# Bonus sums of the RWKV recurrence: both heads and two chunks in one matrix product, in a two-layer trunk on one core

## The chip, the core and the metric

The kernel runs on one core of a Trainium2 chip. A core has a matrix engine (TensorE, PE in the profile; its weight loads are listed apart as PEld), a vector engine (DVE), a scalar engine (ACT), GpSimd (POOL), and DMA queues, here issued by SyncE (SP). The engines run their own instruction lists and wait for each other by semaphores. The metric is the device time of one execution in microseconds (us); lower is better.

## The reference, cut to what matters

A trunk of two layers over 1024 tokens of 1024 features, all in 32-bit floats. Layer 1 is RWKV-7 time mixing, layer 2 a diagonal state-space mixer (S5) with a gated output; each is followed by a dense MLP with 4096 hidden features and a squared ReLU, and each of the four sub-layers ends in a layer norm over `sqrt(2) * h + f(h)`. The change touches one term of the first, the bonus:

```
r, k, v = xr @ wr, xk @ wk, xv @ wv          # xr, xk, ...: x mixed with the token before
kk = heads(k * k_k); kk = kk / max(norm(kk), 1e-12)
k  = k * (1.0 + (a - 1.0) * k_a)             # a: sigmoid of a low-rank product
...
state = state * w_t + (state @ a_t) b_t' + v_t k_t'      # one 64 x 64 state per head, token by token
o_t   = state @ r_t
...
o = group_norm(o) * lnx_g + lnx_b
bonus = sum(rh * kh * r_k, axis=-1, keepdims=True) * vh  # one number per token and head, times v
o = o + bonus
return (o * g) @ wo
```

There are 16 heads of 64 features. The bonus needs, for each of 1024 tokens and 16 heads, one sum over 64 features.

## The kernel before, in words

Activations lie with the features on the 128 partitions (eight tiles of 128) and 512 tokens along the free dimension. The tokens are worked in two halves H = 0 and 1. Every large product is made of three (`mm3`, L204): the high parts of weight and operand, high by low and low by high; `split` makes the high part on ACT (L155) and the low part on DVE (L156). This is the bulk of PE's work: first the projections of both halves (`rwkv_proj`), whose results go to DRAM as `scr["r"]`, `scr["k"]`, `scr["sg"]`, `scr["a"]`, `scr["g"]` and `scr["v"]`, then for H = 0 the output projection `wo(0)`, the first layer norm, and the MLP; then `wo(1)` and so on for H = 1, and the layers behind.

Beside the bulk runs the recurrence, in eight units m = 0 to 7. A unit holds 256 tokens (four chunks of 64) and eight heads (512 features, half q = m % 2), as two pairs of feature tiles, j = 0 and 1. For each unit:

- `elem(m)` loads k, sg, a and r of its tokens (tiles `ldk`, `ldsg`, `lda`, `ldr`), 128 features by 2 x 256 tokens for each j. It squares `kk` on ACT (L549, L550), sums over each head on PE (`pss`, L553), turns the inverse norms back with four transposes (`pn`, L561), runs the scan of the log decays on DVE (L564), two exponentials on ACT, and forms `kf`, `AR` and `KB` (L573 to L584). Then POOL multiplies `kf` by r, and PE makes the **bonus sums** `pb` (L590) with `rksel`, a table that holds r_k of the first head of a tile in its first column, zero on the other head's partitions, and that of the second head in its second column. One DVE copy (L592) takes them to `bo`.
- `amat` makes the products of a chunk's vectors among each other (`pA`, L614), `kbtrans` transposes `KB` (`pT`), `invert` solves the 64 x 64 triangles, and `chain` passes the state from chunk to chunk (`pR`, `pX`, `pU`, `pO`, L718 to L745).
- `gnorm` normalises the result and adds the bonus: POOL multiplies v by `bo` into `vt` (L781) and adds. The sums are thus read one unit later than they are made.

In `bo` the four chunks of the unit lie along the free dimension, beside the four feature tiles; the 64 tokens of a chunk lie on 64 partitions, the upper 64 for the first head of a tile and the lower 64 for the second.

Two PSUM banks (pool `pa`) serve `pss`, `pn`, `pb` and `pA` in turn; three (`pd`) serve the bulk products, two (`pc`) the chain, one (`pl`) the layer norms and `invert`.

**What sets the order.** The engines' lists are fixed when the program is built. Each part gets a base rank (`with rank(...)`): the units m * 10000 with offsets of `RK`, the bulk of half 0 and 1 100000, `wo(0)` 99000, the first layer norm -1. A scheduler goes through all of them with an estimate of each instruction's time and takes at every step what is ready with the lowest rank. So an edit in `elem` can shift every instruction behind it on every engine.

**Other places that the text speaks of.** The first layer norm (`layer_norm` with `by_pe`, half 0): DVE subtracts the mean `pm` from eight tiles `hA` (L927), ACT squares them (L874), PE sums the squares (`pq`), POOL and ACT make the scale `rb` (L896), PE turns it (`pr`, L899), DVE scales (L881) and the parts `oAh` and `oAl` go to the MLP. Behind the first MLP's blocks, `yload(1)` splits the recurrence's result `yl` into `oBh` and `oBl` (L156) for `wo(1)`, the second output projection, whose sums are added to `hB` (L1018); DVE also makes the tables of layer 2 (`s5_tables`, `turns`, L1170 to L1271) there, and adds the MLP's output sums to `hA` (L1050).

Of the kernel before, what the change touches and what calls it, by code (L numbers as in the profile page):

```python
# [20 lines left out]
L = 64  # L21
# [52 lines left out]
def trunk(ctx, tc, A):  # L74
    nc = tc.nc
    V, S, G, PE, SP = nc.vector, nc.scalar, nc.gpsimd, nc.tensor, nc.sync
# [39 lines left out]
    def vec(n, k):  # L116
        i = PV.index(n)
        return pv[:, i, k : k + 1]
# [7 lines left out]
    rksel = kp.tile([128, KT, 2], F32, name="rksel")  # L126
# [393 lines left out]
    def elem(m):  # L520
        D = Unit()
        D.m, D.H, D.q, D.t0 = m, m // 4, m % 2, (m // 2) * 256
        D.KB, D.AR, D.o, D.vsa = [], [], {}, {}
        D.bo = kp.tile([128, NC, NP], F32, tag="bo", name="bo", bufs=3)
        D.PL = kp.tile([128, NC, NP], F32, tag="PL", name="PL", bufs=3)
        for j in range(2):
            n0 = 4 * D.q + 2 * j
            ld = {}
            for nm in ("k", "sg", "a", "r"):
                t = kp.tile([128, 512], F32, tag="ld" + nm, name="ld" + nm, bufs=EB[3] if nm in EB[4] else 1)  # L530
                SP.dma_start(t.rearrange("p (i t) -> p i t", i=2),
                             scr[nm][n0 * 128 : n0 * 128 + 256, D.t0 : D.t0 + 256].rearrange("(i p) t -> p i t", p=128))
                ld[nm] = t
            r, k, cs, a = ld["r"], ld["k"], ld["sg"], ld["a"]

            def v3(t):
                return t.rearrange("p (c l) -> p c l", l=L)

            def per(i):
                return slice(256 * i, 256 * i + 256)  # L540

            def ci(t):
                return t[:, :, 2 * j : 2 * j + 2].rearrange("p c i -> p i c")


            sq = kp.tile([128, HT], F32, tag="sq", name="sq", bufs=EB[0])
            kk = kp.tile([128, HT], F32, tag="kk", name="kk", bufs=EB[1])
            for i in range(2):
                S.mul(kk[:, per(i)], k[:, per(i)], vec("k_k", n0 + i))  # L549
            S.activation(sq, kk, AF.Square)  # L550
            ps = pa.tile([128, HT], F32, tag="a", name="pss")
            for tt in range(4):
                PE.matmul(ps[:, tt * 2 : tt * 2 + 2], sq[:, tt * 128 : (tt + 1) * 128], hsel, start=True, stop=True)  # L553
            rn = kp.tile([128, 8], F32, tag="rn", name="rn", bufs=2)
            V.tensor_scalar(rn, ps[:, 0:8], 1e-24, None, op0=ALU.max)
            G.tensor_tensor(rn, rn, mhalf[:, 0:8], op=ALU.pow)
            rnb = sq.rearrange("p (t h n) -> p t h n", t=4, h=2)
            S.copy(rnb, rn.rearrange("p (t h) -> p t h", h=2).unsqueeze(3).broadcast_to([128, 4, 2, 64]))
            pn = pa.tile([128, HT], F32, tag="a", name="pn")
            for tt in range(4):  # L560
                PE.transpose(pn[:, tt * 128 : (tt + 1) * 128], sq[:, tt * 128 : (tt + 1) * 128], ident)  # L561
            V.tensor_mul(kk, kk, pn)

            V.tensor_tensor_scan(cs, cmask.rearrange("p c l -> p (c l)"), cs, 0.0, op0=ALU.mult, op1=ALU.add)  # L564
            E = kp.tile([128, 8, L + 1], F32, tag="E", name="E", bufs=EB[5])
            G.memset(E[:, :, 0:1], 1.0)
            S.activation(E[:, :, 1:], v3(cs), AF.Exp, scale=-DECAY)
            V.tensor_copy(ci(D.PL), E[:, :, L].rearrange("p (i c) -> p i c", i=2))
            S.activation(cs, cs, AF.Exp, scale=DECAY)

            kf = kp.tile([128, HT], F32, tag="kf", name="kf", bufs=EB[2])
            for i in range(2):
                S.activation(kf[:, per(i)], a[:, per(i)], AF.Identity, bias=kam[:, n0 + i : n0 + i + 1],  # L573
                             scale=kah[:, n0 + i : n0 + i + 1])
            G.tensor_mul(kf, kf, k)
            ar = kp.tile([128, 8, 2, L], F32, tag="AR", name="AR", bufs=ARB)
            kb = kp.tile([128, 8, 2, L], F32, tag="KB", name="KB", bufs=KBB)
            V.tensor_mul(ar[:, :, 1], v3(r), E[:, :, 1:])
            V.scalar_tensor_tensor(ar[:, :, 0], v3(kk), -1.0, E[:, :, 0:L], op0=ALU.mult, op1=ALU.mult)
            V.scalar_tensor_tensor(a, a, 1.0, kk, op0=ALU.add, op1=ALU.mult)  # L580
            for h in range(2):
                hs = slice(64 * h, 64 * h + 64)
                V.tensor_mul(kb[hs, :, 1 - h], v3(kf)[hs], v3(cs)[hs])
                V.scalar_tensor_tensor(kb[hs, :, h], v3(a)[hs], 0.5, v3(cs)[hs], op0=ALU.mult, op1=ALU.mult)  # L584
            G.tensor_mul(kf, kf, r)
            pb = pa.tile([128, HT], F32, tag="a", name="pb")
            for c in range(8):
                for h in range(2):
                    hs, bs = slice(64 * h, 64 * h + 64), slice(64 * (1 - h), 64 * (1 - h) + 64)
                    PE.matmul(pb[bs, c : c + 1], kf[hs, c * L : (c + 1) * L], rksel[hs, n0 + c // 4, h : h + 1],  # L590
                              start=True, stop=True)
            V.tensor_copy(ci(D.bo), pb[:, 0:8].rearrange("p (i c) -> p i c", i=2))  # L592
            D.KB.append(kb)
            D.AR.append(ar)
        return D
# [213 lines left out]
    def core():  # L809
# [4 lines left out]
        with rank(3000):  # L814
            cur = elem(0)
# [6 lines left out]
        for m in range(8):  # L822
# [13 lines left out]
            if m < 7:  # L836
                with rank(base + RK[1]):
                    nxt = elem(m + 1)
# [800 lines left out]
```

## Time and profile before

| what | value |
|---|---|
| three runs | 2599.53, 2601.27, 2612.87 us; median 2601.27 |
| profiled execution, its own time | 2606.15 us |
| its span, first to last instruction | 2604.40 us |
| mean granted clock of TensorE | 0.970 |
| busy: ACT, POOL | 1206.7 us (46%), 400.0 us (15%) |
| bonus products `pb` in the program | 256, in 16 groups of 16 |

All times of single instructions come from the profiled execution. The span is cut into stretches by what the bulk does: up to about 800 us it is the projections, the first output projection and the start of the first MLP block, with the recurrence beside them; to 1030 us the first MLP with the end of the recurrence; to 1300 us the end of that MLP, the second output projection and the tables; then layer 2's half of the work. A busy share says what an engine did, not who waited; for that the chain that ended last and the idle time of a stretch are read together.

### The profile page before, as it was taken

The numbers are of one execution on the slowest core, as the hardware profiler recorded it, in microseconds if no ns is written. First come the engines' busy times: TensorE is split into PE (matmuls) and PEld (weight loads), VectorE is DVE, ScalarE is ACT, GpSimd is POOL, SyncE is SP. The second block draws the span as 40 slices with busy tenths as digits, with TensorE's granted clock in tenths as the row PEclk, the third lists the DMA queues.
The fourth block names the chain that finished last, engine by engine and source line by source line (L and its number), as shares of the span: only waits on it lengthen the run. The fifth ranks groups of instructions, "written<-read, shape, count | busy, mean of one in ns | idle before, by whom it ended". The sixth has DMA issues, their size and how long they took to land.

```text
span 2604.4 us, 43848 instructions
## 1 busy us (share of the span) xinstructions
PE 2478.2 (95%) x16684; PEld 2011.6 (77%) x16684; DVE 1809.7 (69%) x3473; ACT 1206.7 (46%) x2155; POOL 400.0 (15%) x334
## 2 busy tenths in 40 slices
PE   7989989999989999999999999999999999999997
PEld 5778767788767888777777888887777888888876
DVE  7467687578786776999886555776586555555576
ACT  7555575454454443345544333433464333433344
POOL 3110431332211102001000000100212111111011
PEclk9989989999889999999999999999999999999998
DMA  4765555565222324445565333254222111111123
GB/s 149 255 199 175 163 193 182 179 189 156 89 73 76 104 86 130 139 133 155 165 222 173 98 97 94 93 183 140 88 87 76 53 49 49 57 49 53 53 93 114
DMA packets 206290, 319.68 MB, mean 123 GB/s; under 512 B 20096, under 2 KB 80640, under 8 KB 206080
## 3 DMA queue, kind: packets, MB, share of 16 engines
q1 hardware_dynamic: 204928, 314.79, 38.5%
q8 instruction: 131, 2.15, 0.4%
q10 hardware_dynamic: 1152, 2.10, 0.2%
q14 instruction: 79, 0.65, 0.1%
HBM read 252.85 MB, written 63.96 MB: 122 GB/s over the span
## 4 chain that ended last, share of the span: by engine, by line
PE 69%; DVE 14%; DMA 8%; ACT 5%; issue 3%; POOL 1%; SPq 1%; ACTq 0%; DVEq 0%; POOLq 0%
PE d L204 51%; PE d L1087 9%; DVE wlo L156 2%; DMA wraw<-in_mw_dram 2%; PE pA L614 1%; DMA ldsg<-s_sg 1%; ACT whi L155 1%; DVE oAl L156 1%; PE pR L722 1%; PE pq L876 1%; DVE xh L660 1%; DMA s_r<-ev 0%; DMA wraw<-in_glu_dram 0%; DVE KB L584 0%; PE pu L1358 0%
## 5 line engine op out<-in xcount | busy, mean ns | idle before, releaser
L155 ACT CAST whi<-wraw 128x512 fp32r<-128x512 f32 x492 | 304.6, 620 | 646.5 <-PE d L204 426.8
L156 DVE TENSOR_TENSOR wlo<-wraw,whi 128x512 fp32r<-128x512 f32 x492 | 357.2, 727 | 250.6 <-ACT whi L155 245.6
L204 PE MATMUL d<-qbuf,whi 128*128 128x512 f32 (+1 forms) x1344 | 409.7, 387 | 11.4 <-DVE hA L1050 5.7
L204 PE MATMUL d<-oAh,whi 128*128 128x512 f32 (+1 forms) x768 | 310.8, 410 | 13.1 <-ACT ev L435 6.8
L204 PE MATMUL d<-oAh,wlo 128*128 128x512 f32 (+1 forms) x768 | 309.3, 406 | 9.8 <-DVE wlo L156 7.5
L204 PE MATMUL d<-oAl,whi 128*128 128x512 f32 (+1 forms) x768 | 308.4, 403 | 6.6 <-DVE oAl L884 4.4
L204 PEld LDWEIGHTS d<-qbuf,whi 128*128 128x128 f32 x1344 | 244.2, 189 | 66.9 <-DVE hA L1050 9.8
L204 PE MATMUL d<-qbuf,wlo 128*128 128x512 f32 (+1 forms) x672 | 256.0, 383 | 1.0 <-DVE wlo L156 0.9
L204 PE MATMUL d<-oBh,wlo 128*128 128x512 f32 x512 | 202.5, 396 | 3.1 <-DVE wlo L156 2.4
L204 PE MATMUL d<-oBh,whi 128*128 128x512 f32 x512 | 202.6, 396 | 1.4 <-ACT whi L155 1.4
L204 PE MATMUL d<-oBl,whi 128*128 128x512 f32 x512 | 201.0, 393 | 0.0
L204 PEld LDWEIGHTS d<-oAh,whi 128*128 128x128 f32 (+1 forms) x768 | 147.3, 193 | 48.8 <-ACT ev L435 9.1
L204 PEld LDWEIGHTS d<-oAh,wlo 128*128 128x128 f32 (+1 forms) x768 | 147.6, 193 | 44.5 <-DVE wlo L156 9.7
L204 PEld LDWEIGHTS d<-oAl,whi 128*128 128x128 f32 (+1 forms) x768 | 148.0, 193 | 38.6 <-DVE oAl L884 4.8
L204 PE MATMUL d<-qh,wlo 128*128 128x512 f32 x384 | 151.3, 394 | 0.0
L204 PE MATMUL d<-ql,whi 128*128 128x512 f32 x384 | 150.6, 392 | 0.0
L204 PE MATMUL d<-qh,whi 128*128 128x512 f32 x384 | 149.2, 389 | 0.0
L204 PEld LDWEIGHTS d<-qbuf,wlo 128*128 128x128 f32 x672 | 126.5, 189 | 27.5 <-DVE wlo L156 2.4
L1050 DVE TENSOR_TENSOR hB<-hB,d 128x512 f32<-128x512 f32 (+1 forms) x168 | 104.8, 632 | 32.4 <-PE d L204 30.6
L1050 DVE TENSOR_TENSOR hA<-hA,d 128x512 f32<-128x512 f32 x144 | 97.4, 681 | 29.1 <-PE d L204 27.7
L204 PEld LDWEIGHTS d<-oBh,wlo 128*128 128x128 f32 x512 | 96.5, 189 | 26.9 <-DVE wlo L156 3.3
L204 PEld LDWEIGHTS d<-oBh,whi 128*128 128x128 f32 x512 | 96.5, 188 | 23.3 <-ACT whi L155 2.3
(489 smaller groups left out, 5079.3 us busy)
## 6 DMA issues: line engine op xcount, KB each, us to landing
wraw<-in_mw_dram SPq DMA_DIRECT2D x376, 256.0 KB, 2.7
wraw<-in_glu_dram SPq DMA_DIRECT2D x64, 256.0 KB, 2.7
low<-wlo SPq DMA_DIRECT2D x52, 256.0 KB, 2.6
wlo<-low SPq DMA_DIRECT2D x52, 256.0 KB, 3.4
raw<-in_mw_dram SPq DMA_DIRECT2D x48, 256.0 KB, 2.6
wraw<-in_wk_dram SPq DMA_DIRECT2D x32, 256.0 KB, 3.4
wraw<-in_wr_dram SPq DMA_DIRECT2D x32, 256.0 KB, 3.8
wraw<-in_wv_dram SPq DMA_DIRECT2D x32, 256.0 KB, 4.1
```

The source lines that it names most:

```text
L155: S.copy(hi, src)
L156: (e or V).tensor_sub(lo, src, hi.bitcast(F32))
L204: bulk.append((PE.matmul(p, w, x, **kw).ins, x.shape[-1]))
L614: prods.append(PE.matmul(pp[h][:, cc, i], D.KB[j][hs, u].rearrange("p j l -> p (j l)"), D.AR[j][hs, u].rearrange("p j l -> p (j l)"), star ...
L660: V.tensor_add(xv[:, s + 1 : 32, 0:w], xv[:, s + 1 : 32, 0:w], tv)
L722: hop.append(PE.matmul(pR[hs, i], at[:, h, c, i, 0], vsa[:, cl, h, i], start=True, stop=True))
L876: PE.matmul(pq[:, j : j + 1], q[:, j * 128 : (j + 1) * 128], ones_c[:, 0:1], start=k + j == 0, stop=k == KT - 1, skip_group_check=True)
L1050: V.tensor_add(z, z, p)
L1087: PE.matmul(p, w[:, k], x, start=not add and k + j == 0, stop=k == 3 and j == 2, skip_group_check=True)
```

## The change

The products of one group (one unit, one j: 512 tokens of two feature tiles) are made with the whole height of the array. A product takes 128 tokens (two chunks) of `kf` as its stationary side, 128 features high, and both columns of `rksel`; since each column is zero on the other head's partitions, it gives the sums of both heads for two chunks at once. 16 products become four. The sums of chunk e of such a pair then stand on partitions 64e to 64e + 63, for both heads, while `bo` wants head h on partitions 64(1 - h) and up. So the one copy becomes four, by head and chunk: the two that stay on their partitions (e = 1 - h) on DVE, the two that move to the other half on ACT.

```diff
@@ -584,12 +584,15 @@ (elem)
             G.tensor_mul(kf, kf, r)
             pb = pa.tile([128, HT], F32, tag="a", name="pb")
-            for c in range(8):
-                for h in range(2):
-                    hs, bs = slice(64 * h, 64 * h + 64), slice(64 * (1 - h), 64 * (1 - h) + 64)
-                    PE.matmul(pb[bs, c : c + 1], kf[hs, c * L : (c + 1) * L], rksel[hs, n0 + c // 4, h : h + 1],
-                              start=True, stop=True)
-            V.tensor_copy(ci(D.bo), pb[:, 0:8].rearrange("p (i c) -> p i c", i=2))
+            for tt in range(4):
+                PE.matmul(pb[:, 2 * tt : 2 * tt + 2], kf[:, tt * 128 : (tt + 1) * 128], rksel[:, n0 + tt // 2],
+                          start=True, stop=True)
+            pbv = pb[:, 0:8].rearrange("p (i c h) -> p c i h", i=2, c=2)
+            for h in range(2):
+                for e in range(2):
+                    (V.tensor_copy if e == 1 - h else S.copy)(
+                        D.bo[64 * (1 - h) : 64 * (1 - h) + 64, e::2, 2 * j : 2 * j + 2],
+                        pbv[64 * e : 64 * e + 64, :, :, h])
             D.KB.append(kb)
             D.AR.append(ar)
```

The products stand on line 588 of the changed kernel, all four copies on line 593, and each line behind is three further down than before. The built program has 8891 entries on PE in place of 8911, runs of equal rows counted as one.

The first group on PE, behind the transposes `pn` of the same unit and among bulk products (`d`); a row is line, operation, out<-in and the shape of the output:

```order
 L204 MATMUL d<-oS,wlo 128x512
 L561 MATMUL pn<-ident,sq 128x128 x4
-L590 MATMUL pb<-rksel,kf 64x1 x16
+L588 MATMUL pb<-rksel,kf 128x2 x4
 L204 MATMUL d<-stash,whi 128x512 x4
 L204 MATMUL d<-stash,wlo 128x512 x2
```

Here nothing but the group itself is another. From some thirty rows further on the two lists differ nearly everywhere in where a piece of the recurrence stands among the bulk.

The first layer norm, on ACT. Before, around its eight squares (`sq<-hA`), up to the next copy of the chain:

```order
L874 ACTIVATE sq<-hA 128x512 x4
L745 COPY o<-pO 128x256
L767 ACTIVATE osq<-o 128x512
L718 COPY vsa<-st 64x256
L874 ACTIVATE sq<-hA 128x512
L549 ACTIVATE kk<-ldk,pv 128x256 x2
L874 ACTIVATE sq<-hA 128x512 x2
L573 ACTIVATE kf<-lda,kam,kah 128x256 x2
L567 ACTIVATE E<-ldsg 128x8x64
L874 ACTIVATE sq<-hA 128x512
L569 ACTIVATE ldsg<-ldsg 128x512
L724 COPY o<-pR 128x256
```

And in the changed kernel, up to the layer norm's scale `rb`:

```order
L877 ACTIVATE sq<-hA 128x512 x2
L593 COPY bo<-pb 64x2x2
L573 ACTIVATE kf<-lda,kam,kah 128x256 x2
L877 ACTIVATE sq<-hA 128x512 x2
L593 COPY bo<-pb 64x2x2
L877 ACTIVATE sq<-hA 128x512
L732 COPY vsa<-pX 64x256
L558 COPY sq<-rn 128x512
L877 ACTIVATE sq<-hA 128x512 x3
L899 COPY rb<-rs 128x512
```

The copies `o<-pO` and `vsa<-st`, the square `osq`, the products `kk` and the exponential `E` have left the stretch among the squares; the two copies `bo` of a group, a copy `vsa<-pX` and the copy of the inverse norms (L558) have come into it.

The same place on DVE, ahead of the eight subtractions of the mean (`hA<-hA,pm`). Before:

```order
L564 SCALAR_TENSOR_TENSOR ldsg<-cmask,ldsg 128x512
L568 COPY PL<-E 128x2x4
L578 TENSOR_TENSOR AR<-ldr,E 128x8x64
L592 COPY bo<-pb 128x2x4
L555 TENSOR_SCALAR rn<-pss 128x8
L1018 SCALAR_TENSOR_TENSOR hA<-hA,d 128x512
L728 COPY vsa<-pX 64x256
L156 TENSOR_TENSOR wlo<-wraw,whi 128x512
L583 TENSOR_TENSOR KB<-kf,ldsg 64x8x64 x2
L927 TENSOR_TENSOR hA<-hA,pm 128x512 x8
```

And in the changed kernel:

```order
L1021 SCALAR_TENSOR_TENSOR hA<-hA,d 128x512
L583 TENSOR_TENSOR KB<-kf,ldsg 64x8x64
L584 SCALAR_TENSOR_TENSOR KB<-lda,ldsg 64x8x64
L583 TENSOR_TENSOR KB<-kf,ldsg 64x8x64
L584 SCALAR_TENSOR_TENSOR KB<-lda,ldsg 64x8x64
L156 TENSOR_TENSOR wlo<-wraw,whi 128x512
L564 SCALAR_TENSOR_TENSOR ldsg<-cmask,ldsg 128x512
L930 TENSOR_TENSOR hA<-hA,pm 128x512 x8
L568 COPY PL<-E 128x2x4
L578 TENSOR_TENSOR AR<-ldr,E 128x8x64
L555 TENSOR_SCALAR rn<-pss 128x8
L593 COPY bo<-pb 64x2x2 x2
```

The scan of the log decays (L564), behind four `KB` products of the group before, now stands directly ahead of the subtractions; what followed the scan before now follows the subtractions.

DVE ahead of the first sum of the second output projection (`hB<-hB,d`). Before, the rows up to it belong to the rotation table `R`:

```order
L156 TENSOR_TENSOR wlo<-wraw,whi 128x512
L1197 TENSOR_TENSOR R<-bb,b_12905 128x32x4
L1198 TENSOR_TENSOR R<-bb,b_12905 128x32x4
L1178 TENSOR_TENSOR q_12873<-R 128x32
L1179 TENSOR_TENSOR q_12874<-R 128x32
L1180 TENSOR_TENSOR q_12873<-q_12873,q_12874 128x32
L1181 TENSOR_SCALAR q_12873<-q_12873 128x32
L1018 SCALAR_TENSOR_TENSOR hB<-hB,d 128x512
```

In the changed kernel they belong to the powers `pw`, which are made ahead of `R`:

```order
L156 TENSOR_TENSOR wlo<-wraw,whi 128x512
L1253 TENSOR_TENSOR bb<-pw 128x64x2
L1254 TENSOR_TENSOR b_12761<-pw 128x64x2
L1173 TENSOR_TENSOR q_12729<-q_12732 128x32
L1174 TENSOR_TENSOR q_12730<-q_12731 128x32
L1255 TENSOR_TENSOR pw<-bb,b_12761 128x32x2
L1256 TENSOR_TENSOR pw<-bb,b_12761 128x32x2
L1021 SCALAR_TENSOR_TENSOR hB<-hB,d 128x512
```

So some 50 rows of table work that stood ahead of this sum now stand behind it. The projection's last low parts `oBl` on DVE come, in the changed kernel, here:

```order
L156 TENSOR_TENSOR oBl<-yl,oBh 128x512
L1053 TENSOR_TENSOR hA<-hA,d 128x512
L156 TENSOR_TENSOR oBl<-yl,oBh 128x512
L1236 TENSOR_SCALAR q_12730<-q_12728 128x32
L156 TENSOR_TENSOR wlo<-wraw,whi 128x512
L1053 TENSOR_TENSOR hA<-hA,d 128x512
L1240 TENSOR_TENSOR q_12732<-q_12729 128x32
L1237 TENSOR_SCALAR q_12730<-q_12730 128x32
L1053 TENSOR_TENSOR hA<-hA,d 128x512
L156 TENSOR_TENSOR wlo<-wraw,whi 128x512
L1242 TENSOR_SCALAR q_12732<-q_12732 128x32
L1053 TENSOR_TENSOR hA<-hA,d 128x512
```

Three more output sums of the MLP's last block (`hA<-hA,d`) follow the last `oBl` there, where ten followed it before.

## The prediction, made before the changed kernel had run

> **What bounds the kernel now.** I read the page first: busy shares, then the chain that ended last. Then the same engines by stage (columns: stretch, its length, busy us and instruction count of PE, PEld, DVE, ACT and POOL, PE clock, DMA share, GB/s).
>
> ```profile
> PE 2478.2 (95%) x16684; PEld 2011.6 (77%) x16684; DVE 1809.7 (69%) x3473; ACT 1206.7 (46%) x2155; POOL 400.0 (15%) x334
> ...
> PE 69%; DVE 14%; DMA 8%; ACT 5%; issue 3%; POOL 1%; SPq 1%; ACTq 0%; DVEq 0%; POOLq 0%
> ```
> ```profile
> 0.00:800.00 800.00, 722.66 (x6405) 587.99 (x6406) 579.80 (x1312) 445.49 (x822) 205.56 (x187) 0.93 0.52 165
> 800.00:1030.00 230.00, 230.00 (x1798) 184.23 (x1797) 163.59 (x333) 99.77 (x180) 25.14 (x20) 1.00 0.31 93
> ```
>
> PE sets the time: 95% busy, 69% of the chain. Of its 126 us idle (2604.4 - 2478.2), 77.3 lie before 800 us (800 - 722.66), where the clock is also only 0.93. From 800 to 1030 us PE never rests. So the recurrence, which ends about 1030 us, is mostly hidden under bulk products; it costs what it takes from PE, and what its results hold up.
>
> **The bonus sums themselves.** The sixteen groups run between 106 and 790 us. The first, on PE (start, length, name, count of records; a product of this type has two):
>
> ```profile
> 106.28 1.09 PE L590 MATMUL pb<-rksel,kf 64*64 64x1 f32 x32
> 107.31 0.73 PE L204 MATMUL d<-stash,whi 64*128 64x512 f32 x4
> ...
> 115.60 0.95 PE L553 MATMUL pss<-hsel,sq 128*128 128x2 f32 x8
> 116.49 0.73 PE L204 MATMUL d<-stash,whi 64*128 64x512 f32 x3
> ```
>
> Sixteen products hold PE 107.31 - 106.28 = 1.03 us. The new group has exactly the shape of the norm sums `pss` on L553: four products, stationary 128x128, two columns, and those hold PE 116.49 - 115.60 = 0.89 us. So 64 products in place of 256 are not a quarter of the time but 0.14 us less per group: 16 x 0.14 = **-2.2 us**. Over all groups, PE's busy time (left of the bar the tiles, right of it busy us and mean ns) says the same from another side:
>
> ```profile
> L590 PE MATMUL pb<-rksel,kf 64*64 64x1 f32 x512 | 20.2, 201 | 4.1 <-POOL kf L585 4.1
> ...
> L553 PE MATMUL pss<-hsel,sq 128*128 128x2 f32 x128 | 18.7, 267 | 0.9 <-ACT sq L550 0.9
> ```
>
> 20.2 - 18.7 is 1.5 us. Ends: -1.5 and -2.2; I take -2.2, from the pair that is nearest in place and clock.
>
> "TensorEngine Tiling (Array Packing)" in the Trainium skill, section "Instruction Overhead", would give more: each matmul has about 60 cycles of overhead, and one with free dimension 1 takes as long as one with 60. By that rule the cost goes by the count of products. The trace disagrees: 64 ns for an old product (1.03 / 16), 222 ns for a `pss` one (0.89 / 4).
>
> **The copies.** One DVE copy becomes two on DVE and two on ACT:
>
> ```profile
> L724 ACT COPY o<-pR 128x256 f32<-128x256 f32 x24 | 8.8, 368 | 7.1 <-PE pR L722 7.0
> ...
> L592 DVE COPY bo<-pb 128x8 f32<-128x8 f32 x16 | 2.6, 162 | 0.1
> ```
>
> DVE: 16 copies more at 0.16 us, +2.6 us. ACT: 32 copies, at DVE's 0.16 us +5, and at the 0.37 of its 256 columns +12. Before 800 us ACT is busy 445 us and DVE 580 of the 800, so on the end they cost nothing unless something waits behind them; the sums themselves are read much later, by POOL's `vt`.
>
> What is new is a handover: an ACT copy, then both DVE copies, which wait for it, then the other ACT copy, which waits for them. "PSUM — Partial Sum Buffer" in the Trainium skill, section "PSUM bank collisions raise a hardware error", says that two engines must not access one bank and 32-partition quadrant at the same time, so the four may not run side by side; no run here shows a collision. In series they are 4 x 0.16 = 0.6 us plus handovers, against 0.16. Queued behind the waiting ACT copy are weight casts `whi` and evacuations `ev`, for which PE waits; behind the DVE copies, `KB` or low parts of weights. In the new order nothing ahead of the first ACT copy or the DVE copies needs a PE result that is over 1 us later than the sums, so I take 0. Ends: 0 and +8, 0.5 us in each group, the length of such a series.
>
> **What the new order moves.** The build places everything anew; two places look large enough to price.
>
> *First layer norm.* DVE subtracts the mean from eight tiles, ACT squares them, PE sums, and DVE scales:
>
> ```profile
> 693.32 1.12 PE L925 MATMUL pm<-hA,ones_c 128*128 128x512 f32 x2
> ```
> ```profile
> 685.13 0.68 DVE L584 SCALAR_TENSOR_TENSOR KB<-lda,ldsg 64x512 f32<-64x512 f32 x1
> ...
> 689.84 1.22 DVE L564 TENSOR_TENSOR_SCAN ldsg<-cmask,ldsg 128x512 f32<-128x512 f32 x1 [2.32 <-DMA ldsg<-s_sg]
> ...
> 697.50 4.87 DVE L927 TENSOR_TENSOR hA<-hA,pm 128x512 f32<-128x512 f32 x8
> ...
> 721.77 5.36 DVE L881 SCALAR_TENSOR_TENSOR hA<-hA,pv,pr 128x512 f32<-128x512 f32 x8 [0.59 <-PE pr L899]
> ```
> ```profile
> 704.26 0.41 ACT L718 COPY vsa<-st 64x256 f32<-64x256 f32 x1 [2.82 <-DVE st L736]
> ...
> 707.17 0.91 ACT L549 ACTIVATE kk<-ldk,pv 128x256 f32<-128x256 f32 x2 [1.97 <-DVE lda L580]
> ...
> 712.44 1.09 ACT L573 ACTIVATE kf<-lda,kam,kah 128x256 f32<-128x256 f32 x2 [3.32 <-DMA lda<-s_a]
> ...
> 713.96 0.61 ACT L874 ACTIVATE sq<-hA 128x512 f32<-128x512 f32 x1
> ```
>
> The last square starts 16.5 us after the first subtraction (713.96 - 697.50), because ACT waits 2.82 + 1.97 + 3.32 = 8.1 us for recurrence work that stands among the squares. In the new order these three waits are gone. But the scan now stands ahead of the subtractions, behind four `KB` products (2.7 us), and its load starts only when they free the tile: 4.0 us (689.84 - 685.81), then 1.2 of scan, 7.9 in all where 4.2 pass today (697.50 - 693.32). So -8.1 + 3.7 = -4.4. PE loses cover: sixteen `pA` products that fill this gap (two times 1.16 us at full clock) come after it.
>
> ```profile
> 733.37 1.16 PE L614 MATMUL pA<-AR,KB 64*128 64x128 f32 x16
> ```
>
> Net -4.4 + 2.3 = **-2.1**; ends -8.1 and +3.7.
>
> *Behind the second output projection.* Against the bulk the last recurrence steps stand 90 products later, 20 us at 0.226 (21.00 / 93 below). So DVE starts the tables of layer 2 later; those that ran from 1064 to 1084 us now come after the projection's first sum.
>
> ```profile
> 1064.00:1084.00 20.00, 20.00 (x87) 15.87 (x86) 19.25 (x69) 7.35 (x13) 0.00 (x0) 1.00 0.34 104
> ...
> 1064.00:1084.00 20.00, 6.80 (x10) 0.00 (x0) 1.00 0.34 104
> ...
> 1064.00:1084.00 20.00, 5.42 (x8) 1.00 0.34 104
> ```
> ```profile
> 1079.00:1100.00 21.00, 21.00 (x93) 17.24 (x92) 18.72 (x49) 4.92 (x8) 3.52 (x2) 1.00 0.28 89
> ```
> ```profile
> 1100.00:1200.00 100.00, 94.56 (x505) 73.64 (x504) 94.68 (x155) 51.03 (x93) 9.86 (x7) 1.00 0.47 129
> ```
>
> The first fence is all engines, then the low parts on DVE (6.80 us), then DVE's output sums (5.42): the tables are 19.25 - 12.2 = 7.0 us. They land where DVE has 5.3 us free in 100 (100 - 94.68), and where PE already idles 5.4 (100 - 94.56). Excess 7.0 - 5.3 = 1.7, **+2**; ends 0 and +7.
>
> There the projection's last operand also comes closer to its use: in the new order three output sums of six products stand behind its split on DVE, and it is first read 21 products into the projection: 39 x 0.226 = 8.8 us of margin. I charge nothing; it is what a late recurrence eats first.
>
> **Sum.** -2.2 + 0 - 2.1 + 2 = -2.3 us. The profiled execution took 2606.15 (span 2604.40 and 1.75 around it), so 2603.9; it lies 4.9 above the median of the runs, 2601.27, so on their scale 2599. A measurement of this kernel can tell about 0.5% (13 us) from no change; this is well inside.
>
> **Rivals.**
>
> *The norm gap closes in full.* In its 29 us PE's clock is 0.62:
>
> ```profile
> 702.00:731.00 29.00, 24.05 (x140) 21.50 (x140) 22.12 (x41) 14.06 (x25) 7.81 (x7) 0.62 0.14 42
> ```
>
> ACT's 8.1 us go, the scan's load hides, `pA` finds other cover, and of the 11 us lost to the clock (0.38 x 29) the share 8.1 / 29 goes too, 3 us: -2.2 - 8.1 - 3 = -13, 2588, faster. For it: the waits are gone from ACT's queue. Against: the load cannot start before `KB` is done.
>
> *DVE becomes the bound behind the second projection.* The 7.0 us of tables fall on PE whole, the operand overruns its 8.8 us margin by 5, and the handover costs 3: 7 + 5 + 3 - 2.2, about +13, 2614, slower. It decides from where the added DVE work exceeds the 5.3 us free and the recurrence runs over 9 us behind the order's plan. For it: DVE is at 95% there, and PE idles. Against: the excess is 1.7.
>
> *The handover stalls* 0.5 us in each of 16 groups: +8 - 2.3, 2607; no change still.
>
> *Cost goes by count*: a quarter of 1.03, so 16 x 0.77 = -12.4 where the forecast has -2.2: 2589, just inside no change. Against: the `pss` rows. That the count doesn't fall is excluded by the order.
>
> **How the numbers follow.** Forecast, 2599: 0.60; handover 0.06; by count 0.04: together 0.70 within 0.5%. Norm gap in full 0.13, faster; DVE bound 0.17, slower. The terms' low ends give -2.2 - 8.1 = -10, 2591; the high ends -1.5 + 3.7 + 7 + 8 = +17, 2618. With the faster rival on the one side and the slower on the other: 2585 to 2617.
>
> **What would show it.** 64 products `pb`, a group in 0.9 us; ACT's copies near 0.16 us; the norm's scaling some 24 us after `pm`; more of DVE's tables behind the second projection, and PE's idle time from 1100 to 1200 us up by 2; no wait for a copy `bo` over 1 us. It is wrong if PE's idle time before 800 us moves by over 10 us at places not named here, since the order differs nearly everywhere.

## The result

The changed kernel takes 2614.53 us (median of 9 runs, 2611.47 to 2622.39), the kernel before 2603.15 in the same comparison (9 runs). The ratio is 1.0055, with a 95% interval of 1.0042 to 1.0068: **slower by half a per cent**. Measured once more, beside other kernels on another chip (12 runs), it was 1.0032 (1.0016 to 1.0047). So the change costs 0.3 to 0.6%, 8 to 14 us, where the forecast was a gain of 2.3 us and no measurable change.

The page of the changed kernel, busy shares and chain:

```profile
PE 2476.4 (95%) x16300; PEld 2013.2 (77%) x16300; DVE 1813.4 (69%) x3489; ACT 1213.8 (46%) x2187; POOL 405.8 (16%) x334
...
PE 71%; DVE 14%; DMA 7%; ACT 4%; issue 3%; POOL 1%; SPq 0%; ACTq 0%; DVEq 0%; POOLq 0%
```

PE is busy 1.8 us less than before (2478.2 - 2476.4), which is about what the products were to save, but the span is 10.6 us longer (2615.0 - 2604.4). So all of the loss is idle time of PE, and the view by stage says where. Of the changed kernel:

```profile
0.00:800.00 800.00, 726.38 (x6042) 590.92 (x6043) 578.86 (x1306) 454.25 (x858) 206.88 (x187) 0.93 0.52 165
...
1100.00:1200.00 100.00, 89.14 (x469) 69.76 (x469) 98.04 (x168) 51.62 (x94) 10.41 (x7) 1.00 0.42 116
1200.00:1300.00 100.00, 90.71 (x514) 70.54 (x511) 81.00 (x128) 49.37 (x92) 12.53 (x6) 0.97 0.61 177
...
765.71:1665.65 899.94, 868.13 (x5565) 699.00 (x5565) 663.95 (x1283) 383.76 (x681) 66.37 (x47) 0.99 0.41 125
```

And of the kernel before, the two rows not shown yet:

```profile
1200.00:1300.00 100.00, 98.31 (x613) 75.86 (x610) 85.50 (x135) 54.51 (x100) 7.99 (x6) 1.00 0.58 161
...
769.18:1653.11 883.93, 869.05 (x5616) 698.33 (x5617) 654.04 (x1257) 381.48 (x675) 62.40 (x47) 0.99 0.42 128
```

The last row of each fence runs between two marks that both programs have: the first low part of the MLP's hidden tile (`qbuf`) and the first Tanh of the gated output. Up to the first mark the changed kernel is 3.5 us ahead (769.2 and 765.7), behind the second it gains 1.9 more. Between them it takes 16.0 us longer (899.94 - 883.93), with PE's busy time the same within 1 us. PE's idle time between the marks is 16.9 us more (31.81 against 14.88); 13.0 of these lie from 1100 to 1300 us (20.15 against 7.13), and most of the rest from 1300 to 1420 us.

So nothing was lost where the bonus sums are made, between 100 and 800 us. The loss lies 300 us behind them, after the second output projection, where the tables of layer 2 are made. What PE waits for from 1030 to 1420 us, in the view of waits (total, times, longest), before:

```profile
PE d L204 <- DVE hA L1050: 4.3, 6, 1.2
...
PE pk L1319 <- DVE ca L1308: 1.1, 1, 1.1
...
PE d L204 <- ACT rl L1033: 0.6, 1, 0.6
```

and after:

```profile
PE d L204 <- DVE hA L1053: 10.6, 7, 2.9
...
PE d L204 <- ACT rl L1036: 3.7, 2, 3.4
PE pk L1322 <- DVE ca L1311: 3.4, 2, 1.9
PE d L204 <- ACT whi L155: 2.4, 2, 2.1
```

PE waits for DVE: for the MLP's output sums `hA`, which give a PSUM bank free, and for the tables themselves (`ca`). These two rows are 8.6 us more than before; ACT's `rl` and `whi` are 4.9 more. Most of `rl` is a single event of this execution: one square of the next norm took 5.74 us on POOL, ACT waited for it, and PE for ACT (rows of POOL, ACT, ACT and PE).

```profile
1258.46 5.74 POOL L940 TENSOR_TENSOR sq<-sq,sq 128x512 f32<-128x512 f32 x1 [31.15 <-ACT sq L939]
...
1264.24 0.63 ACT L939 ACTIVATE sq<-hA 128x512 f32<-128x512 f32 x1 [4.82 <-POOL sq L940]
1264.77 0.58 ACT L1036 ACTIVATE rl<-d 128x512 f32<-128x512 f32 x1
...
1265.40 0.73 PE L204 MATMUL d<-qbuf,whi 128*128 128x512 f32 x2 [3.37 <-ACT rl L1036]
```

In a second profile of the same program (e17 below) that square takes 2.08 us and the longest wait for `rl` is 0.7; there the stretch between the marks is 10.8 us longer than before, not 16.0.

DVE's timeline shows what has changed there: the first table row and the last one ahead of the projection's first sum `hB`. Before, 95 records with 20.8 us in all:

```profile
1033.77 0.09 DVE L1240 MEMSET pw<- 128x32 f32 x1
...
1084.67 0.18 DVE L1181 TENSOR_SCALAR q<-q 128x32 f32<-128x32 f32 x1
1084.77 0.68 DVE L1018 SCALAR_TENSOR_TENSOR hB<-hB,d 128x512 f32<-128x512 f32 x1
```

After, 41 records with 7.8 us:

```profile
1049.65 0.09 DVE L1243 MEMSET pw<- 128x32 f32 x1 [0.23 <-DMA s_y<-gt]
...
1081.26 0.23 DVE L1256 TENSOR_TENSOR pw<-bb,b 128x64 f32<-128x64 f32 x1
1081.40 0.68 DVE L1021 SCALAR_TENSOR_TENSOR hB<-hB,d 128x512 f32<-128x512 f32 x1
```

The projection comes at about the same time, but the tables start 16 us later, since the recurrence ends later against the bulk. 13.0 us of table work that stood ahead of the projection (20.8 - 7.8) now stand behind it.

What goes with it is seen at the norm that follows the projection, where DVE subtracts the mean from eight tiles in one piece. Before, PE has products of finished tables (`pk`) to make in that time (PE alone):

```profile
1138.57 0.83 PE L1319 MATMUL pk<-ca,bb 64*16 64x128 f32 x10
...
1142.92 0.74 PE L204 MATMUL d<-qbuf,whi 128*128 128x512 f32 x2 [0.59 <-DVE hA L1050]
```

After, the first such product stands 64 bulk products further on in PE's list, and even there it waits for its table. So PE waits for the sum behind the subtractions (DVE's row, then PE's rows):

```profile
1132.48 4.86 DVE L930 TENSOR_TENSOR hB<-hB,pm 128x512 f32<-128x512 f32 x8
...
1138.00 0.73 PE L204 MATMUL d<-qbuf,whi 128*128 128x512 f32 x2 [2.89 <-DVE hA L1053]
...
1148.83 1.90 PE L1322 MATMUL pk<-ca,bb 64*16 64x128 f32 x30 [1.57 <-DVE ca L1311]
```

Late tables can hence cost in two ways: DVE still has their work to do, and PE lacks their products as cover. The last experiments try to part the two.

### The profile page after: what moved, and what is told of

It is laid out like the page before. It is cut to its first block, busy times and chain, and to the rows that moved or that the text cites. A ratio compares the mean times of both kernels' runs of the same rounds, so it can differ in the third digit from the quotient of the medians.

```text
span 2615.0 us, 43143 instructions
## 1 busy us (share of the span) xinstructions
PE 2476.4 (95%) x16300; PEld 2013.2 (77%) x16300; DVE 1813.4 (69%) x3489; ACT 1213.8 (46%) x2187; POOL 405.8 (16%) x334
## 4 chain that ended last, share of the span: by engine, by line
PE 71%; DVE 14%; DMA 7%; ACT 4%; issue 3%; POOL 1%; SPq 0%; ACTq 0%; DVEq 0%; POOLq 0%
PE d L204 53%; PE d L1090 9%; DVE wlo L156 2%; DMA wraw<-in_mw_dram 2%; PE pA L617 1%; ACT whi L155 1%; DVE oAl L156 1%; DMA wraw<-in_wv_dram 1%; DMA ldsg<-s_sg 1%; DMA lda<-s_a 1%; PE pR L725 1%; DMA s_y<-yg 1%; PE pU L735 1%; PE pX L730 1%; PE pq L879 1%
```

## The experiments

**T**, the theory: the loss is the place of the tables; the bonus only shifted the order. Two rivals stand against it: **P**, the products or copies themselves, and **H**, the handover between ACT and DVE at each group. "Rows ahead" are the rows of table work on DVE ahead of the first sum of the second output projection, 98 before and 44 after, read off the order.

### Parts of the change, and the projection moved without it

Products alone, one copy as before:

```diff
-            pbv = pb[:, 0:8].rearrange("p (i c h) -> p c i h", i=2, c=2)
-            for h in range(2):
-                for e in range(2):
-                    (V.tensor_copy if e == 1 - h else S.copy)(
...
+            V.tensor_copy(ci(D.bo), pb[:, 0:8].rearrange("p (i c) -> p i c", i=2))
```

> The new products, but one DVE copy as before; it leaves out the placing of the sums in the right half (the bonus term comes out misplaced). Built so, 98 rows of table work stand ahead of the first sum of the second output projection on DVE, as in the kernel before (44 in the changed kernel). Theory T (the loss is table work of layer 2 that comes to stand behind that sum, where DVE is full): 2598 to 2603 us, the gain of the products at most 2.2 us. Rival P (the products themselves, or the place that they take, cost the 11 us): about 2614.

Measured: 0.9989 (0.9977 to 1.0002), some 3 us less, though the interval still holds no gain at all. That is what T had, and it fits the size that the forecast gave the products.

Copies alone, the old products with one copy cut in two:

```diff
-            V.tensor_copy(ci(D.bo), pb[:, 0:8].rearrange("p (i c) -> p i c", i=2))
+            for h in range(2):
+                V.tensor_copy(D.bo[64 * h : 64 * h + 64, :, 2 * j : 2 * j + 2].rearrange("p c i -> p i c"),
+                              pb[64 * h : 64 * h + 64, 0:8].rearrange("p (i c) -> p i c", i=2))
```

> The old 256 products, but two DVE copies of 64 partitions in place of one of 128; nothing on ACT, no handover, all results right. Built so, 44 rows of table work stand ahead of the first sum of the second output projection, as in the changed kernel. T: 2612 to 2618 us, although only 16 copies of 0.16 us were added. Rival P (products) and rival H (the handover between ACT and DVE at each group): 2603, at most 2.6 more.

Measured: 1.0119 (1.0103 to 1.0135), 31 us: over twice what T had. 16 copies of 0.16 us are 2.6 us, so the greater part must come with the new order. In its trace the mark at the MLP's first hidden tile stands at 801.2 us (769.2 before), and the stretch ahead of it has less PE and less clock than that of the kernel before (722.66 and 0.93):

```profile
0.00:800.00 800.00, 711.44 (x6217) 574.49 (x6218) 546.46 (x1228) 434.95 (x800) 199.36 (x179) 0.91 0.51 161
```

Between the marks it takes 895.9 us, 12 more than before. So a shuffled order can cost time ahead of that mark too, and T has nothing to say on that part; what it waits for there was not followed up. In the changed kernel that part came out even.

The second output projection one MLP block later in the changed kernel, and one earlier in the kernel before:

```diff
-INS1 = 12
+INS1 = 13     # e3, in the changed kernel
+INS1 = 11     # e4, in the kernel before
```

> The whole change, with the second output projection placed one MLP block later (INS1 = 13): 102 rows of table work stand ahead of its first sum, and its operands are ready 216 bulk products ahead of their use (210 in the kernel before, 120 in the changed one). T: 2598 to 2604 us. Rivals P and H: still about 2614.

> The kernel before, with the second output projection placed one MLP block earlier (INS1 = 11): 42 rows of table work stand ahead of its first sum. T: 2612 to 2618 us without any of the change. Rivals P and H: 2603, give or take 3.

Measured: 0.9998 (0.9988 to 1.0008) and 1.0031 (1.0015 to 1.0047). The loss goes with the distance between tables and projection, in a kernel that has none of the change as well (8 us in e4, a little under what T had). Both runs move the margin of the projection's operands too, but in e4's trace PE waits for no operand there from 1000 to 1130 us; its longest wait, 5.4 us, is for `hA` behind the subtractions.

### The tables delayed, relieved, and the copies placed otherwise

The kernel before, with the tables held back:

```diff
-        V.tensor_scalar(lr, lr, -1e-4, None, op0=ALU.min)
+        inorder([sums[87], V.tensor_scalar(lr, lr, -1e-4, None, op0=ALU.min)])
...
-                        V.tensor_add(z, z, p)
+                        sums.append(V.tensor_add(z, z, p))
```

> The kernel before with one thing more: the first product of the tables of layer 2 on DVE may not be placed ahead of the last sum of the MLP's block 11. PE's list is that of the kernel before up to entry 3535, where the tables begin; 48 rows of table work stand ahead of the first sum of the second output projection (98 before, 44 in the changed kernel). T: 2612 to 2618 us, with the whole loss between 1100 and 1400 us of the trace. If the loss of the changed kernel came from its products, its copies or the recurrence's new places: 2603, give or take 3.

Measured: 1.0040 (1.0025 to 1.0055), median 2611.83. No bonus, no copy and no step of the recurrence was touched, and a loss of 10 us is there, as large as that of the changed kernel. Its trace has PE idle 18.5 us from 1100 to 1420 us, against 11.5 in the kernel before, and the longest wait stands behind the same subtractions:

```profile
1143.60 1.22 PE L204 MATMUL d<-qbuf,whi 128*128 128x512 f32 x2 [5.01 <-DVE hA L1050]
```

32 of the table products on POOL, in the changed kernel and in the one before:

```diff
-                    V.tensor_mul(w[:, :, ri], pi_, y[:, ri, gs].unsqueeze(2).broadcast_to(sh4))
+                    G.tensor_mul(w[:, :, ri], pi_, y[:, ri, gs].unsqueeze(2).broadcast_to(sh4))
```

> The changed kernel with the 32 products tw of the tables on POOL in place of DVE (21.8 us of DVE's time in its trace); all ahead of the tables is as in the changed kernel. T (DVE is the bound behind the second output projection): 8 to 13 us less than the changed kernel, 2602 to 2607. If DVE isn't what PE waits for there, or POOL's share of the memory port gives it back: 2612 to 2616.

> The same 32 products on POOL in the kernel before. T: DVE has less over its free time there, so the gain is smaller than that of the changed kernel: 0 to 6 us, 2597 to 2603.

Measured: 1.0046 (1.0028 to 1.0064) and 1.0021 (1.0008 to 1.0035). T failed in both: the relief brought the changed kernel little, and made the other slower. The trace of the first has PE idle only 11.9 us from 1100 to 1300 us, 8 less than the changed kernel, but at a clock of 0.95 and 0.97 in the two halves, and DVE's low parts of weights take 805 ns in the mean (699 in the changed kernel) while POOL multiplies. It moves the load, and says nothing clean.

All four copies on DVE; three on DVE and one on ACT; all four on ACT:

```diff
-                    (V.tensor_copy if e == 1 - h else S.copy)(
+                    V.tensor_copy(                                               # e8
+                    (S.copy if (h, e) == (1, 1) else V.tensor_copy)(             # e9
+                    S.copy(                                                      # e10
```

> The new products with all four copies on DVE, so without the handover between ACT and DVE; 44 rows of table work stand ahead of the first sum of the second output projection, as in the changed kernel. T: 2611 to 2618 us. Rival H (the handover costs, one group of it held PE up for 5.4 us in the changed kernel's trace): 2604 to 2609.

> The whole change with three of the four copies on DVE and one on ACT. The order that the build makes of it has 98 rows of table work ahead of the first sum of the second output projection, as in the kernel before (44 with two and two, and with four on DVE). T: 2597 to 2604 us, as little as the products alone. If the loss comes from the products, from more copies on DVE, or from the handover: 2610 to 2618.

> The whole change with all four copies on ACT; 84 rows of table work stand ahead of the first sum. T: a loss in proportion, about a quarter of that of the changed kernel, so 2603 to 2609 us. Otherwise no forecast.

Measured: 1.0067 (1.0048 to 1.0085), 1.0004 (0.9991 to 1.0016) and 1.0020 (1.0005 to 1.0035), with 44, 98 and 84 rows ahead. The same change costs 0.7%, nothing, or 0.2%, in the order of the rows ahead. H falls with e8.

### Less table work

`tw` and the sums with it left out, in the changed kernel and in the one before:

```diff
-                    V.tensor_mul(w[:, :, ri], pi_, y[:, ri, gs].unsqueeze(2).broadcast_to(sh4))
-                V.tensor_add(dst[:, :, :, 1:], dst[:, :, :, 1:], w)
```

> The changed kernel without the second half of the tables' products: tw and the 16 sums with it are left out (layer 2's tables come out without their cross terms), some 40 us of DVE's work behind the second output projection. T: with DVE no longer full there, the changed kernel is as fast as the kernel before with the same left out, within 4 us. If DVE isn't the bound: 11 to 14 us slower than that.

> The kernel before with the same products and sums left out. T: faster than the kernel before by what its PE waits for DVE there, some 4 to 8 us; the changed kernel with the same left out is within 4 us of it. If DVE isn't the bound: no gain.

Measured: 1.0052 (1.0034 to 1.0070) and 1.0002 (0.9991 to 1.0013): the first is 13 us slower than the second, and the second gains nothing. T failed in both, and both came as was written for the case that DVE isn't the bound. But the build had moved the order again; layer 2's own products came 150 places later in the first. So the pair cannot part load from order, and led to the runs with a fixed order.

### The order held

Here a table of the wanted order of every engine goes into the kernel, and each instruction is bound to stand behind the one ahead of it, without a wait. The old bonus's 16 products, or the new one's four, take the place of the first product of the other's group; the DVE copies take the place of the last DVE copy; what the ACT copies have no place for is left free.

```diff
+        for x, y in zip(seq, seq[1:]):
+            tc.add_manual_dep(y, x.name, mybir.DependencyInfo(
+                mybir.DependencyClass.NoSync, mybir.DependencyReason.DATA), reason="order")
```

> The old 256 products and one copy, with every other instruction of every engine in the order of the changed kernel (16 groups in the place of the new ones). Theory O (the order carries the whole loss): 2611 to 2618 us, 0.4 to 0.7% over the kernel before. If the new products or copies carry it: 2600 to 2605.

> The new 64 products and four copies, with every other instruction of every engine in the order of the kernel before. O: 0 to 3 us under the kernel before, by the 2.2 us of the products less what the handover costs. If the products or copies carry the loss: 8 to 14 us over it.

Measured: 1.0026 (1.0012 to 1.0040) and 1.0004 (0.9991 to 1.0016). The old bonus is slower in the new order (by 0.26%, where O had 0.4 to 0.7); the new one costs nothing that shows in the old. PE's idle time from 1100 to 1300 us goes with the order: 6.2 us in e14,

```profile
1100.00:1200.00 100.00, 95.19 (x491) 74.81 (x490) 94.49 (x157) 50.10 (x93) 11.05 (x9) 1.00 0.44 124
1200.00:1300.00 100.00, 98.62 (x558) 75.62 (x557) 87.96 (x140) 55.10 (x101) 8.35 (x6) 1.00 0.58 156
```

as in the kernel before (7.1). Since 0.26% is less than the 0.55% of the changed kernel on another chip, both were run side by side:

> The changed kernel as it is, beside the next one on the same chip. O (the order carries all): within 3 us of the next. If the copies' handover carries a part: 5 to 8 us above the next.

> The old bonus in the changed kernel's order once more. O: within 3 us of the changed kernel, 7 to 14 us over the kernel before. If the copies' handover carries a part: 5 to 8 us below the changed kernel.

Measured: 1.0032 (1.0016 to 1.0047) and 1.0027 (1.0015 to 1.0040). They are equal within the intervals: **the order carries the loss**, and products, copies and handover carry none that shows. The upper end of e14's interval leaves them 4 us at most. The trace of e18 has PE idle 12.1 us there, and a clock of 0.95:

```profile
1100.00:1200.00 100.00, 92.20 (x474) 72.23 (x473) 98.05 (x162) 51.45 (x94) 10.41 (x7) 0.95 0.45 124
1200.00:1300.00 100.00, 95.73 (x647) 74.77 (x646) 87.17 (x139) 52.40 (x97) 9.32 (x6) 1.00 0.63 183
```

Less table work once more, now with all other instructions in their places:

> The changed kernel in its own order, with the products tw of the tables and the 16 sums with them left out (48 instructions, some 40 us of DVE's time behind the second output projection); all others keep their places. Theory D (PE waits there since DVE is full): 8 to 15 us less than the changed kernel, PE's idle time from 1100 to 1300 us under 10 us in place of 20.2. If DVE's load is not what PE waits for: at most 3 us less.

> The kernel before in its own order with the same 48 instructions left out. D: 3 to 7 us less than the kernel before, whose PE idles 7.1 us from 1100 to 1300 us, so that the two kernels come within 4 us of each other. If DVE's load is not what PE waits for: no gain, and the 11 us between the two stay.

Measured: 1.0005 (0.9995 to 1.0016) and 0.9988 (0.9977 to 1.0000). On the same chip the changed kernel's order stood at 1.0026 with its full load (e13) and that of the kernel before at 1.0004 (e14). So with 40 us less for DVE both orders get faster, by some 5 and 4 us. They stay 0.17%, 4.4 us, apart, where they were 0.22% apart with the full load; the intervals can't tell the two distances from each other. D's gain of 8 to 15 us for the changed order isn't reached, nor is its rival's 3 or less; its gain for the kernel before is at the low end, and its distance of within 4 us is just missed. PE's idle time from 1100 to 1300 us falls to 8.8 us in e15, as D had it,

```profile
1100.00:1200.00 100.00, 94.61 (x511) 73.34 (x510) 84.10 (x146) 54.23 (x99) 9.18 (x7) 1.00 0.45 124
1200.00:1300.00 100.00, 96.60 (x640) 76.97 (x639) 72.58 (x121) 52.45 (x98) 9.22 (x6) 0.98 0.65 187
```

but it falls in e16 as well, to 3.8:

```profile
1100.00:1200.00 100.00, 96.70 (x522) 75.47 (x521) 78.21 (x130) 55.18 (x101) 9.25 (x7) 1.00 0.48 133
1200.00:1300.00 100.00, 99.49 (x652) 77.38 (x651) 72.64 (x121) 51.13 (x93) 7.93 (x6) 1.00 0.63 186
```

Between the two marks of the result, e15 and e16 take 887.1 and 877.8 us, 9.3 apart; with the full load e18 and e14 take 893.6 and 885.8, 7.8 apart. And PE's wait behind the subtractions is still there in e15, where DVE is busy 84% of the 100 us in place of 98:

```profile
1135.85 0.73 PE L204 MATMUL d<-qbuf,whi 128*128 128x512 f32 x2 [2.74 <-DVE hA L1053]
```

So DVE's load costs time in both orders, but it is not shown to be what parts them. That late tables leave PE without products to cover its waits, and start layer 2 later, fits what is left; it was not tried by itself.

No version that keeps the whole computation beats the kernel before: e3, e9 and e14 equal it. e1 and e16, 3 us under it, leave something out.

## Why the prediction was wrong, step by step

- **The products, -2.2 us: right.** The first group holds PE 0.95 us against 1.09, and a group stays near the four `pss` products that it was priced by:

```profile
105.30 0.95 PE L588 MATMUL pb<-rksel,kf 128*128 128x2 f32 x8
```

  Over all groups PE is busy 17.8 us with them, where it was 20.2:

```profile
L588 PE MATMUL pb<-rksel,kf 128*128 128x2 f32 x128 | 17.8, 256 | 4.1 <-POOL kf L585 4.1
```

  e1 gives -3 us (-6 to +0.5). The rival by count, -12.4, is excluded by both.

- **The copies at nothing: right in the sum, wrong in its reason.** ACT's copies take 157 ns and DVE's 160 in the mean, near the 0.16 that was the lower price. The prediction looked ahead of the copies for late results of PE alone. In one group DVE's copies stood behind a scan that waited for a load (ACT's first copy, DVE's scan and copies, ACT's last copy, then PE, which needs the bank):

```profile
516.69 0.15 ACT L593 COPY bo<-pb 64x4 f32<-64x4 f32 x1
520.94 1.23 DVE L564 TENSOR_TENSOR_SCAN ldsg<-cmask,ldsg 128x512 f32<-128x512 f32 x1 [5.16 <-DMA ldsg<-s_sg]
522.20 0.33 DVE L593 COPY bo<-pb 64x4 f32<-64x4 f32 x2
523.35 0.16 ACT L593 COPY bo<-pb 64x4 f32<-64x4 f32 x1
523.56 1.86 PE L617 MATMUL pA<-AR,KB 64*128 64x128 f32 x13 [5.41 <-ACT bo L593]
```

  PE idled 5.41 us for a copy, where the prediction said that no wait for `bo` would exceed 1 us. It cost nothing that shows in the end: e17 and e18, with and without the handover, are equal within some 5 us, and e8 without it is no faster.

- **The first layer norm, -2.1: near in its sum, by luck, and wrong in its parts.** The prediction had the scaling some 24 us behind `pm`, where it stood 28.5 behind it before (721.77 - 693.32). It comes 25.5 us behind it (710.33 - 684.87):

```profile
684.87 1.02 PE L928 MATMUL pm<-hA,ones_c 128*128 128x512 f32 x2
```
```profile
687.55 4.84 DVE L930 TENSOR_TENSOR hA<-hA,pm 128x512 f32<-128x512 f32 x8
...
710.33 5.36 DVE L884 SCALAR_TENSOR_TENSOR hA<-hA,pv,pr 128x512 f32<-128x512 f32 x8 [1.70 <-PE pr L902]
```

  So -3.0 where -4.4 was counted. But the scan ahead of the subtractions, +3.7, cost nothing: from `pm` to the first subtraction it is 2.7 us (4.2 before). And the three waits on ACT, -8.1, were worth little: from the first subtraction to the scaling it takes 22.8 us (710.33 - 687.55), 24.3 before (721.77 - 697.50), -1.5. The two errors cancel. Whether this gain reached the end can't be told: the mark at the first hidden tile stands at 765.7 and 771.5 us in two profiles of the very same program.

- **The tables of layer 2, +2 (0 to +7): this step failed.** That tables would move behind the second output projection was named rightly; the size was not: between the marks it is +16.0 us in the first profile, of which some 5 go with the slow square on POOL (3.4 us of wait, and a lower clock behind it), and +10.8 in that of e17 (894.69 - 883.93). PE's idle time from 1100 to 1200 us, which was to rise by 2, rose by 5.4 (10.86 against 5.44). Late tables alone cost 10.4 us in e5. Two things went into the wrong size. First the work displaced: the prediction counted only what DVE did on tables in the last 20 us ahead of the projection, 7.0 us; what moved were the 13.0 us between 20.8 and 7.8. The order, which stood in the text, already had it: 98 - 44 = 54 rows, at some 0.24 us each. Second the price: it set this work against DVE's mean free time, 5.3 us in 100. That this is the measure is not borne out, since the two orders stay 4.4 us apart with 40 us less work on DVE. PE's longest waits for DVE stand behind one piece of work, the eight subtractions, and the tables' products that covered it there before are gone. How much of the loss is the missing cover, and how much layer 2 starting later, stays open.

- **The margin of the projection's operand, 8.8 us, charged 0: right.** No product of `wo(1)` waits for `oBl` there.

- **The rivals.** The one that came nearest is the second, DVE as the bound behind the second projection, and its 2614 is the time measured. That is luck: it had it from three parts (tables 7, operand 5, handover 3) of which the last two didn't occur, DVE's load as the bound is not borne out by e15 and e16, and its chance of 0.17 was set against an excess of 1.7 us that was the same mis-sized term. The range, 2585 to 2617, held the time.

## What to carry to other kernels

Where a scheduler places the program, an edit is two changes: what it costs by itself, and the new order. Price the second by the position of whole stages (here rows ahead of the next stage, 98 or 44), since the same edit cost from 0 to 0.7% by where three tiny copies were put, and two copies alone cost 1.2%. When an edit comes out slower far from its own place, hold the order fixed before you blame or undo it. And don't price work that is pushed into a later stage by that stage's mean free time: look at which piece of work the waiting engine stands behind, and what it had as cover there.

## What the runs showed of the hardware

One wait of PE can cost more than its length. In e18 PE idles 3.27 us, and then works at half its clock for some 10 us. PE's row, then the view by 4 us (the clock is the third column from the end):

```profile
1134.42 1.22 PE L204 MATMUL d<-qbuf,whi 128*128 128x512 f32 x2 [3.27 <-DVE hA L1050]
```
```profile
1132.00:1136.00 4.00, 1.58 (x4) 1.29 (x5) 4.00 (x7) 2.13 (x5) 1.28 (x1) 0.68 0.00 0
1136.00:1140.00 4.00, 3.49 (x9) 2.30 (x8) 4.00 (x8) 1.96 (x4) 0.00 (x0) 0.50 0.00 0
1140.00:1144.00 4.00, 4.00 (x11) 3.11 (x11) 4.00 (x7) 1.70 (x3) 1.27 (x1) 0.54 0.18 66
1144.00:1148.00 4.00, 3.69 (x39) 2.84 (x38) 4.00 (x6) 0.70 (x2) 0.87 (x1) 1.00 0.63 192
```

The three slow rows lose 4 x (0.32 + 0.50 + 0.46) = 5.1 us of clock, most of it behind the wait. But the length of a wait doesn't tell whether this happens. At the same place in the changed kernel's first profile PE waited 2.89 us, and its clock stayed at 1.00 over the 100 us; a wait of 2.08 us further on in that profile was followed by a clock of 0.60:

```profile
1296.15 1.56 PE L204 MATMUL d<-qbuf,whi 128*128 128x512 f32 x4 [2.08 <-ACT whi L155]
```
```profile
1296.00:1300.00 4.00, 3.85 (x10) 3.06 (x11) 1.93 (x3) 4.00 (x8) 0.00 (x0) 0.60 0.29 79
```

So the sum of the waits alone, 12.1 us in e18 and 20.15 in the changed kernel, doesn't tell the price. "TensorE: Matmul & The Clock Gate" in the Trainium skill, part 1, "What's actually happening", says that the clock falls to one half after an idle window of about 3.4 us, and that the windows run freely. The half agrees with these traces (0.50); the length does not, since a wait of 2.08 us is shorter than that window.

The prediction cited "TensorEngine Tiling (Array Packing)" in the Trainium skill, "Instruction Overhead", for a price by count. The changed kernel's own group, 0.95 us for four products against 1.09 for sixteen, and e1's -3 us speak against it for these small products in 32-bit floats.
